# Delta rule: the products that complete the triangular inverse stand directly behind its blocks, ahead of the layout of queries and values and the grams

## The chip, the cores and the metric

The program runs on one core of one Trainium2 chip. The metric is device time in microseconds (us) of one execution. The engines are TensorE (PE, its weight loads PEld), VectorE (DVE), ScalarE (ACT), GpSimd (POOL) and SyncE (SP, which here issues the weight DMAs). Each runs its own instructions in its own fixed order and waits for the others by semaphores.

## The reference

One sequence of 256 tokens, width 1024, fp32, passes two blocks of two layers each. The first (differential attention with latent attention, then a dense network or a mixture of experts) isn't touched by the change. A layer of the second has grid attention beside a gated delta rule in both directions (8 heads, key and value width 64, chunks of 64 tokens), then a gated network with a convolution:

```python
k_beta = k * beta[..., None]
a_kk = where(strict, einsum("bhnid,bhnjd->bhnij", k_beta, k) * decay, 0.0)
t_inv = triangular_solve(eye + a_kk, eye, left_side=True, lower=True, unit_diagonal=True)
u = t_inv @ (v * beta);   w = t_inv @ (k_beta * exp(gcum))
qk = einsum("bhnid,bhnjd->bhnij", q, k) * decay
def step(state, inp):                     # over the chunks, in order
    v_new = ui - wi @ state
    o = qd @ state + qki @ v_new
    state = state * gt + kd.T @ v_new
```

q and k are normalised per head before (`l2norm`), and the two directions' outputs are added.

## The kernel before

A tile framework turns the Python code into one instruction list per engine. The order of the code is the priority; a list scheduler then places each instruction on its engine, by a model of times, when its inputs and its buffer are due. So the order on an engine is fixed before the run, isn't the order of the code, and can change far from an edit. PSUM tiles come from small rings: tag `sd` has 3 banks, `at` 2, `mm` 2, `ex` 1, and tiles of a tag are handed out in the order of the code.

The second block's weights stream in as 1 MB tiles `raw`. Most of its products are feature groups: `feat_group` multiplies a weight tile with the transposed activations `xf` in fp32 (L541, out `mm` or `ex`), or with split halves (L546 to L548). They depend on little and stand between everything else on PE.

`mix2` builds one mixer layer and steps through the generator `delta` with four calls of `next(dn)`, the last two directly behind each other (L1407, L1408). Behind them it writes down `dn_out` (which transposes the delta rule's output `O` into `odT`, L381 and L376/L377), the gates' groups (L541), the attention's output groups (on `oaT`) and the delta rule's (on `odT`).

`delta` goes, in the code's order, through these stages:

- decays and their exponentials; key layout and norm; per pair of heads (`hp`, 4 of them) the gram of the keys, and `apply` (L1680) which multiplies it into the decay matrix `Ma`;
- the inverse of all 64 x 64 unit triangles at once, on DVE: diagonal blocks of 32 are inverted by doubling and two closing passes (L1753, L1754), and two transposes (L1757) lay the blocks out as `xo`; copies bring them to `Wm` (L1762) and `Wc` (L1765), on ACT and DVE;
- weights of `qk` and `kd` on POOL;
- the part that the change moves (L1781 to L1788): `tok_layout(0)` and `tok_layout(2)` (transposes of `cT` on PE, copies on ACT, L1622), `l2norm(0, 0.125)` (queries: reductions L1629, small steps up to L1633 and products L1636 on DVE, transposes `cv` on PE, copies `qkT` L1640), and per pair of heads the gram of queries and keys and `apply` with `qk` on POOL (L1680);
- the loop that completes the inverse (L1789 to L1824): per pair of heads the tiles L1 (copies and transposes of `Ma`) and L2 (copies of `xo`, L1804), four products psY (L1808), the copy Yc (L1810, DVE), four products psZ (L1814), and the writing of the inverse into `Ma` (copies L1820, and psZ, L1823, L1824). psZ's products need Yc, and psY and psZ are `sd` tiles;
- `vf`, state and buffer clears (xv, L1836), and the recurrence: 16 pairs (hp, chunk), each a chain of products (L1865, L1887), copies and sums (L1860), staggered. L1665 and L1673 in the code are gram and its copies.

At the same time the grid attention runs in pieces, two heads at a time: scores (L1489), maximum (L1493), exponential `e` (L1498), transposes (L381), products (L1510), `ob` (L1514), and its transposes into `oaT` (L376, L377). Below, a step of a product group with its wait is written with the line that it has in this kernel; behind the change the lines L1789 to L1824 are 8 lower (L1808 is L1800, L1810 is L1802, L1814 is L1806, L1820 is L1812, L1801 is L1793, L1799 is L1791, L1804 is L1796).

Of the kernel before, what the change touches and what calls it, by code (L numbers as in the profile page):

```python
# [11 lines left out]
F32 = mybir.dt.float32  # L12
# [10 lines left out]
NT = 2  # L23
# [162 lines left out]
class Net:  # L186
# [1147 lines left out]
    def mix2(s, l):  # L1334
# [92 lines left out]
        for g in range(4):  # L1427
# [5 lines left out]
            nc.vector.tensor_tensor(out=v, in0=v, in1=m[:, gs, :], op=OP.add)  # L1433
            t = s.reg.tile([128, 2, 2, 256], F32R, tag=("E1", "E2", "KQ", "CV")[g], name="mT")
            s.split(t[:, 0], t[:, 1], v)
# [105 lines left out]
    def delta(s, l, cT, zb, sv, hg):  # L1541
        nc = s.nc
# [4 lines left out]
        reg, sm = s.reg, s.sm  # L1547
# [69 lines left out]
        def tok_layout(b3):  # L1617
            for tt in range(NT):
                pt = s.ps([128, 4, 128], "sd")
                for cc in range(4):  # L1620
                    s.tr(pt[:, cc], cT[b3 // 2][:, 4 * b3 % 8 + cc, tt * 128:tt * 128 + 128])
                nc.scalar.copy(cv[:, tt, b3].rearrange("p h d -> p (h d)"), pt.rearrange("p c d -> p (c d)"))  # L1622

        def l2norm(b3, scale):
            ss = sm.tile([128, NT, 8, 1], F32, tag="nss", name="nss")
            for tt in range(NT):
                j = s.tmp.tile([128, 8, 64], F32, tag="l0", name="j", bufs=2)
                nc.scalar.activation(j, cv[:, tt, b3], AF.Square)
                nc.vector.reduce_sum(ss[:, tt, :, 0], j, axis=AX.X)  # L1629
            TS(ss, ss, 4e-6, None, op0=OP.add)  # L1630
            r = s.rsqrt(ss, [128, NT, 8, 1])
            if scale != 1.0:
                TS(r, r, scale, None, op0=OP.mult)  # L1633
            for tt in range(NT):
                v = cv[:, tt, b3]
                T(out=v, in0=v, in1=r[:, tt].to_broadcast([128, 8, 64]), op=OP.mult)  # L1636
                pt = s.ps([128, 4, 128], "sd")
                for cc in range(4):
                    s.tr(pt[:, cc], cv[:, tt, b3, 2 * cc:2 * cc + 2].rearrange("p h d -> p (h d)"))
                nc.scalar.copy(qkT[:, b3, :, tt * 128:tt * 128 + 128], pt)  # L1640
# [9 lines left out]
        qk = reg.tile([128, 4, 4, 2, 64], F32, tag="qk", name="qk")  # L1650
# [13 lines left out]
        def gram(hp, w, out):  # L1664
            ps = [s.ps([128, 2, 128], "sd") for _ in range(2)]  # L1665
            for tt in range(NT):
                for h2 in range(2):
                    bs = slice(64 * h2, 64 * h2 + 64)
                    ts = slice(tt * 128, tt * 128 + 128)
                    mm(ps[h2][:, tt], lhsT=qkT[bs, 1, hp, ts], rhs=qkT[bs, w, hp, ts], start=True, stop=True)  # L1670
            for h2 in range(2):
                for hf in range(2):
                    nc.scalar.copy(out[H[hf], :, h2], ps[h2][H[hf], :, 64 * hf:64 * hf + 64])  # L1673

        def apply(d, kk, eng=nc.vector):
            for hf in range(2):
                for tt in range(NT):
                    n0 = (0, 1)[tt] if hf == 0 else (1, 0)[tt]
                    ns = slice(n0, 4, 3) if n0 == 0 else slice(1, 3)
                    eng.tensor_tensor(out=d[H[hf], ns], in0=kk[H[hf], tt:tt + 1].to_broadcast([64, 2, 2, 64]),  # L1680
                                      in1=d[H[hf], ns], op=OP.mult)
# [92 lines left out]
        for hp in range(4):  # L1774
            for hf in range(2):
                bw = ((1, 1), (3, 0)) if hf == 0 else ((0, 1), (2, 0))
                for ns, ts, k in ((slice(hf, 4, 2), slice(0, 2), 2),
                                  *((slice(n, n + 1), slice(t, t + 1), 1) for n, t in bw)):
                    PT(out=kd[H[hf], hp, ns], in0=cv[H[hf], ts, 1, h2s(hp)],
                       in1=eT[H[hf], ns, h2s(hp)].to_broadcast([64, k, 2, 64]), op=OP.mult)  # L1780
        tok_layout(0)  # L1781
        l2norm(0, 0.125)
        tok_layout(2)
        KQ = reg.tile([128, 4, NT, 2, 64], F32, tag="KQ", name="KQ")
        for hp in range(4):
            gram(hp, 0, KQ[:, hp])
            apply(qk[:, hp], KQ[:, hp], nc.gpsimd)
        yield  # L1788
        Ls = [reg.tile([128, 2, 2, 2, 128], F32, tag=tag, name="L") for tag in ("E1", "E2")]  # L1789
        for x in Ls:  # L1790
            nc.gpsimd.memset(x, 0.0)  # L1791
# [1 line left out]
        for hp in range(4):  # L1793
            hs = h2s(hp)
            L1, L2 = (x[:, hp % 2] for x in Ls)
            M = Ma[:, hp]  # L1796
            for hf in range(2):
                r0 = 64 * hf
                nc.scalar.copy(L1[r0 + 32:r0 + 64, :, :, r0:r0 + 32], M[r0 + 32:r0 + 64, hf::2, :, 0:32])  # L1799
                for n in (1 - hf, 3 - hf):  # L1800
                    nc.vector.transpose(out=L1[r0:r0 + 32, n // 2, :, r0 + 32:r0 + 64],  # L1801
                                        in_=M[r0 + 32:r0 + 64, n, :, 0:32])  # L1802
            for i in range(4):
                copies[i](L2[R32[i], :, :, 32 * i:32 * i + 32], xs(1, R32[i], i in (1, 2))[:, :, hs])  # L1804
            psY = s.ps([128, 2, 2, 32], "sd")
            for n in range(2):  # L1806
                for h2 in range(2):
                    mm(psY[:, n, h2], lhsT=L1[:, n, h2], rhs=Wm[:, n, 2 * hp + h2], start=True, stop=True)  # L1808
            Yc = s.tmp.tile([128, 2, 2, 32], F32, tag="m0", name="Yc")
            cp(Yc, psY)  # L1810
            psZ = s.ps([128, 2, 2, 32], "sd")
            for n in range(2):  # L1812
                for h2 in range(2):
                    mm(psZ[:, n, h2], lhsT=L2[:, n, h2], rhs=Yc[:, n, h2], start=True, stop=True)  # L1814
            for hf in range(2):
                r0 = 64 * hf
                nc.vector.memset(M[r0 + 32:r0 + 64, hf::2, :, 0:32], 0.0)
                nc.vector.memset(M[r0:r0 + 32, 1 - hf::2, :, 32:64], 0.0)
            for i in range(4):
                copies[i](M[R32[i], :, :, 32 * (i % 2):32 * (i % 2) + 32], Wc[R32[i], :, hs])  # L1820
            for hf in range(2):
                r0 = 64 * hf
                TS(M[r0:r0 + 32, hf::2, :, 32:64], psZ[r0:r0 + 32], -1.0, None, op0=OP.mult)  # L1823
                nc.scalar.mul(M[r0 + 32:r0 + 64, 1 - hf::2, :, 0:32], psZ[r0 + 32:r0 + 64], -1.0)  # L1824
        s.O = s.const.tile([128, NT, 8, 64], F32, tag="O", name="O")
        vf = reg.tile([128, NT, 8, 64], F32, tag="C4", name="vf")
        for tt in range(NT):
# [211 lines left out]
```

## Time and profile before

| | us |
|---|---|
| time, median of 3 runs (lowest to highest) | 2782.64 (2781.74 to 2784.24) |
| the profiled execution's own time | 2780.29 |
| its span, first to last instruction | 2778.5 |
| PE busy / PEld busy | 2668.2 (96%) / 2294.7 (83%) |
| DVE / ACT / POOL busy | 2081.2 (75%) / 1642.9 (59%) / 339.1 (12%) |
| mean granted clock of PE | 0.982 |

The delta rule stands in the span twice, at about 1855 to 2050 us and 2335 to 2530 us. A busy share is a mean over very different stages, so the stretches are read apart; a clock of 1.00 is full speed (2.4 GHz) and 0.50 half of it (1.2 GHz). In a row of the timeline the bracket at the end tells how long the engine stood idle before the instruction, and whose result ended that.

### The profile page before, as it was taken

The page shows a single profiled execution, that of the slowest core. Times are in us where ns is not written, and L with a number is a line of the kernel's source. Part 1 is how long each engine was busy: PE and PEld are TensorE (multiplying, and loading weights), DVE is VectorE, ACT ScalarE, POOL GpSimd, SP SyncE. Part 2 cuts the span into 40 slices and gives each one's busy share as a digit, 9 for nine tenths or more (in the row PEclk, how much of TensorE's full clock was granted, in tenths as well). Part 3 has the DMA queues.
Part 4 walks back from the last instruction along what each step waited for, and adds up shares of the span by engine and source line. Part 5 has one row for each costly group of instructions (what it writes and reads, how often), then busy time and mean ns, then how long its engine had stood idle before and what let it go on. Part 6 is the DMA issues. An engine that isn't in the chain of part 4 may idle for free. (4 is left out here: it accounts for less than half of the span.)

```text
span 2778.5 us, 41248 instructions
## 1 busy us (share of the span) xinstructions
PE 2668.2 (96%) x15729; PEld 2294.7 (83%) x15729; DVE 2081.2 (75%) x3322; ACT 1642.9 (59%) x2557; POOL 339.1 (12%) x360
## 2 busy tenths in 40 slices
PE   8999999899999999999999999989999999999999
PEld 7988998798887888788787878767788987777997
DVE  7576654647779989898988988869487856947784
ACT  5564543456467777777777777625555533455563
POOL 3324000132400000000000000024210003321000
PEclk9999999999989999999999999989999999999999
DMA  6335554433669999998999999532235543213553
GB/s 221 121 122 189 197 185 173 158 137 131 242 239 359 353 348 361 359 355 338 358 357 339 355 366 346 216 127 93 77 108 197 183 168 123 92 61 133 176 187 136
DMA packets 92939, 610.31 MB, mean 220 GB/s; under 512 B 13627, under 2 KB 14473, under 8 KB 22977
## 3 DMA queue, kind: packets, MB, share of 16 engines
q1 hardware_dynamic: 89968, 601.34, 58.8%
q0 software_dynamic: 2768, 6.28, 0.9%
q8 instruction: 126, 2.06, 0.3%
q14 instruction: 77, 0.62, 0.1%
HBM read 606.56 MB, written 1.05 MB: 219 GB/s over the span
## 5 line engine op out<-in xcount | busy, mean ns | idle before, releaser
L305 DVE TENSOR_TENSOR wl<-raw,wh 128x1024 fp32r<-128x1024 f32 (+1 forms) x938 | 1130.2, 1224 | 314.4 <-ACT wh L303 292.1
L303 ACT CAST wh<-raw 128x1024 fp32r<-128x1024 f32 (+1 forms) x996 | 1028.0, 1043 | 564.7 <-PE mm L342 162.4
L341 PE MATMUL mm<-wl,xg 128*128 128x512 f32 x896 | 354.8, 396 | 1.3
L340 PE MATMUL mm<-wh,xg 128*128 128x512 f32 x896 | 351.8, 395 | 0.0
L342 PE MATMUL mm<-wh,xg 128*128 128x512 f32 x896 | 351.1, 392 | 0.0
L547 PE MATMUL mm<-xTl,wh 128*128 128x256 f32 x1040 | 298.7, 287 | 0.0
L546 PE MATMUL mm<-xTh,wh 128*128 128x256 f32 x1040 | 297.6, 286 | 0.0
L548 PE MATMUL mm<-xTh,wl 128*128 128x256 f32 x1040 | 295.9, 285 | 0.4 <-DVE wl L305 0.4
L341 PEld LDWEIGHTS mm<-wl,xg 128*128 128x128 f32 x896 | 168.3, 188 | 42.4 <-DVE wl L305 7.4
L546 PEld LDWEIGHTS mm<-xTh,wh 128*128 128x128 f32 x1040 | 198.4, 191 | 1.9 <-issue 1.3
L548 PEld LDWEIGHTS mm<-xTh,wl 128*128 128x128 f32 x1040 | 198.7, 191 | 1.0 <-DVE wl L305 0.8
L340 PEld LDWEIGHTS mm<-wh,xg 128*128 128x128 f32 x896 | 168.3, 188 | 36.3
L547 PEld LDWEIGHTS mm<-xTl,wh 128*128 128x128 f32 x1040 | 197.7, 190 | 0.5
L342 PEld LDWEIGHTS mm<-wh,xg 128*128 128x128 f32 x896 | 168.3, 188 | 35.7
L305 POOL TENSOR_TENSOR wl<-raw,wh 128x1024 fp32r<-128x1024 f32 x58 | 143.0, 2466 | 332.8 <-ACT wh L303 324.8
L342 PE MATMUL sd<-wh,ac 128*128 128x512 f32 x448 | 175.6, 392 | 0.0
L341 PE MATMUL sd<-wl,ac 128*128 128x512 f32 x448 | 175.5, 392 | 0.0
L541 PE MATMUL mm<-xf,raw 128*128 128x256 f32 (+1 forms) x704 | 148.3, 361 | 0.0
L340 PE MATMUL sd<-wh,ac 128*128 128x512 f32 x448 | 144.2, 395 | 0.0
L541 PEld LDWEIGHTS mm<-xf,raw 128*128 128x128 f32 x704 | 119.0, 194 | 17.1 <-issue 3.7
L796 POOL DMA_DIRECT2D gb<-in_ln_ffn_g_dram x2 | 1.1, 561 | 971.6 <-DMA raw<-in_w_dram 971.3
L303 ACT CAST ww<-raw 128x1024 fp32r<-128x1024 f32 x74 | 77.2, 1047 | 67.2 <-PE mm L548 21.0
(627 smaller groups left out, 5452.4 us busy)
## 6 DMA issues: line engine op xcount, KB each, us to landing
raw<-in_w_dram SPq DMA_DIRECT2D x545, 1024.0 KB, 4.9
raw<-in_w_dram SPq DMA_DIRECT2D x24, 512.0 KB, 3.5
raw<-in_w_dram SPq DMA_DIRECT2D x8, 576.0 KB, 4.0
raw<-in_w_dram SPq DMA_DIRECT2D x8, 544.0 KB, 3.5
raw<-in_w_dram SPq DMA_DIRECT2D x4, 768.0 KB, 5.9
xt<-in_x_dram SPq DMA_DIRECT2D x2, 512.0 KB, 3.7
gb<-in_ln_mix_g_dram POOLq DMA_DIRECT2D x2, 512.0 KB, 4.9
gb<-in_ln_mix_b_dram POOLq DMA_DIRECT2D x2, 512.0 KB, 7.8
```

The costliest lines, as they stand in the source:

```text
L303: s.nc.scalar.copy(r[0], raw)
L305: eng.tensor_tensor(out=r[1], in0=raw, in1=r[0].bitcast(F32), op=OP.subtract)
L340: mm(out, lhsT=lh, rhs=rh, start=start, stop=False)
L341: mm(out, lhsT=lh, rhs=rl, start=False, stop=False)
L342: return mm(out, lhsT=ll, rhs=rh, start=False, stop=stop)
L541: mm(o[:, t], lhsT=h[:, kk, sl], rhs=xh[:, kk, t], start=kk == 0, stop=kk == k - 1)
L546: mm(o, lhsT=h[:, kk, sl], rhs=xh[:, kk, :], start=kk == 0, stop=False)
L547: mm(o, lhsT=h[:, kk, sl], rhs=xl[:, kk, :], start=False, stop=False)
L548: mm(o, lhsT=l[:, kk, sl], rhs=xh[:, kk, :], start=False, stop=kk == k - 1)
L796: s.nc.gpsimd.dma_start(gb[:, 0], row_bc(s.A[nm + "_g"], i * D, D))
```

## The change

The block of `delta` that lays out queries and values, normalises the queries and forms the grams of queries and keys moves behind the loop that completes the inverse. Nothing is added or left out.

```diff
@@ -1778,14 +1778,6 @@
                     PT(out=kd[H[hf], hp, ns], in0=cv[H[hf], ts, 1, h2s(hp)],
                        in1=eT[H[hf], ns, h2s(hp)].to_broadcast([64, k, 2, 64]), op=OP.mult)
-        tok_layout(0)
-        l2norm(0, 0.125)
-        tok_layout(2)
-        KQ = reg.tile([128, 4, NT, 2, 64], F32, tag="KQ", name="KQ")
-        for hp in range(4):
-            gram(hp, 0, KQ[:, hp])
-            apply(qk[:, hp], KQ[:, hp], nc.gpsimd)
-        yield
         Ls = [reg.tile([128, 2, 2, 2, 128], F32, tag=tag, name="L") for tag in ("E1", "E2")]
@@ -1822,6 +1814,14 @@
                 r0 = 64 * hf
                 TS(M[r0:r0 + 32, hf::2, :, 32:64], psZ[r0:r0 + 32], -1.0, None, op0=OP.mult)
                 nc.scalar.mul(M[r0 + 32:r0 + 64, 1 - hf::2, :, 0:32], psZ[r0 + 32:r0 + 64], -1.0)
+        tok_layout(0)
+        l2norm(0, 0.125)
+        tok_layout(2)
+        KQ = reg.tile([128, 4, NT, 2, 64], F32, tag="KQ", name="KQ")
+        for hp in range(4):
+            gram(hp, 0, KQ[:, hp])
+            apply(qk[:, hp], KQ[:, hp], nc.gpsimd)
+        yield
         s.O = s.const.tile([128, NT, 8, 64], F32, tag="O", name="O")
```

How this stands on the engines is taken from the two instruction lists. The first place is PE in the first layer, from the transpose of an attention block (`ob`) at the end of the inverse on. Before, feature groups and the transposes of the normalised queries (`cv`) and of `cT` follow:

```order
L381 MATMUL at<-ident,ob 128x128 [waits DVE_49]
L1489 MATMUL at<-AT 128x256 [waits PE_49]
L1489 MATMUL at<-AT 128x256
L541 MATMUL mm<-xf,raw 128x256 x4
L541 MATMUL ex<-xf,raw 128x256
L381 MATMUL sd<-ident,cv 128x128 [waits DVE_49]
L381 MATMUL sd<-ident,cv 128x128 x3
L381 MATMUL sd<-ident,cv 128x128 [waits DVE_49]
L381 MATMUL sd<-ident,cv 128x128 x3
L381 MATMUL sd<-ident,cT 128x128 x4
L541 MATMUL ex<-xf,raw 128x256 x9
```

With the change, from the same transpose on, psY (on `Wa` and `L`) and psZ (on `Yc`):

```order
L381 MATMUL at<-ident,ob 128x128 [waits DVE_49]
L1489 MATMUL at<-AT 128x256 [waits PE_49]
L1489 MATMUL at<-AT 128x256
L1800 MATMUL sd<-Wa,L 128x32 [waits DVE_49,Activation_49,Pool_49]
L1800 MATMUL sd<-Wa,L 128x32 x3
L1806 MATMUL sd<-Yc,L 128x32 [waits DVE_49,Activation_49,Pool_49]
L1806 MATMUL sd<-Yc,L 128x32 x3
L1800 MATMUL sd<-Wa,L 128x32 x4
L381 MATMUL at<-ident,e 128x128 [waits PE_49,Activation_49]
L381 MATMUL at<-ident,e 128x128
L381 MATMUL at<-ident,e 128x128 [waits Activation_49]
L381 MATMUL at<-ident,e 128x128
```

The four psY products and the four psZ products of the first pair now stand directly behind the attention's scores; the feature groups and the layout have gone behind all four pairs.

The second place is DVE in the same stretch, from the last copies into `Ma` on; before:

```order
L1820 COPY Ma<-Wa 32x8x32 x3
L1820 COPY Ma<-Wa 32x8x32 [waits DVE_49]
L1820 COPY Ma<-Wa 32x8x32 x3
L1493 TENSOR_REDUCE gnm<-at 128x2 [waits PE_49]
L377 TENSOR_TENSOR oaT<-at,oaT 128x4x128 [waits Activation_49]
L1495 TENSOR_TENSOR gnm<-gnm,gr 128x2 [waits DVE_49]
L1512 RECIPROCAL gsum<-gsum 128x2 [waits Activation_49]
```

With the change:

```order
L1812 COPY Ma<-Wa 32x8x32 x3
L1812 COPY Ma<-Wa 32x8x32 [waits DVE_49]
L1812 COPY Ma<-Wa 32x8x32 x3
L1493 TENSOR_REDUCE gnm<-at 128x2 [waits PE_49]
L1793 STREAM_TRANSPOSE L<-Ma 32x2x32 [waits PE_49]
L1793 STREAM_TRANSPOSE L<-Ma 32x2x32
L377 TENSOR_TENSOR oaT<-at,oaT 128x4x128 [waits Activation_49]
L1495 TENSOR_TENSOR gnm<-gnm,gr 128x2 [waits DVE_49]
L1802 COPY Yc<-sd 128x128 [waits PE_49]
L1793 STREAM_TRANSPOSE L<-Ma 32x2x32 x2
```

Yc of the first pair, which stood far behind the attention's steps, now comes behind the split of the attention's output (`oaT`, L377) and its small step L1495.

The third place is ACT beside it, from the last copies of the blocks on; before:

```order
L1804 COPY L<-xo 32x4x32 x2
L1820 COPY Ma<-Wa 32x8x32 x3
L376 CAST oaT<-at 128x4x128 [waits PE_49]
L1820 COPY Ma<-Wa 32x8x32 [waits DVE_49]
L1820 COPY Ma<-Wa 32x8x32 x3
L1417 ACTIVATE m<-mm 128x512 [waits PE_49]
L1640 COPY qkT<-sd 128x4x128 [waits PE_49] x2
```

With the change:

```order
L1796 COPY L<-xo 32x4x32 x2
L1812 COPY Ma<-Wa 32x8x32 x3
L1812 COPY Ma<-Wa 32x8x32 [waits DVE_49]
L1812 COPY Ma<-Wa 32x8x32 x3
L376 CAST oaT<-at 128x4x128 [waits PE_49]
L1791 COPY L<-Ma 32x4x32 [waits PE_49]
L1791 COPY L<-Ma 32x4x32
```

The cast to `oaT` (L376), for which DVE's L377 waits, stood between the copies into `Ma` and now stands behind all eight; the copies of `qkT` are gone from here.

The last place is PE behind the delta rule of the first layer, where its output `O` is transposed for the products on `odT`; before:

```order
L381 MATMUL sd<-ident,O 128x128 [waits DVE_49,Pool_49]
L381 MATMUL sd<-ident,O 128x128 [waits Pool_49] x3
L546 MATMUL mm<-oaT,wh 128x256
L547 MATMUL mm<-oaT,wh 128x256
L381 MATMUL sd<-ident,O 128x128 [waits DVE_49]
L381 MATMUL sd<-ident,O 128x128 x3
L548 MATMUL mm<-oaT,wl 128x256
```

With the change:

```order
L548 MATMUL mm<-oaT,wl 128x256
L381 MATMUL sd<-ident,O 128x128 [waits DVE_49,Pool_49]
L381 MATMUL sd<-ident,O 128x128 [waits Pool_49] x3
L381 MATMUL sd<-ident,O 128x128 [waits DVE_49]
L381 MATMUL sd<-ident,O 128x128 x3
L546 MATMUL ex<-odT,wh 128x256 [waits Activation_49]
L546 MATMUL mm<-odT,wh 128x256 [waits PE_49] x2
L547 MATMUL ex<-odT,wh 128x256 [waits DVE_49]
```

Before, products on `oaT` stand between and behind the two groups of transposes; now all eight transposes stand together, and the first products on `odT` directly behind them.

Behind it, 21 products L541 stand between the recurrence's first products in the first layer, where 1 stood before. The order of the weight DMAs on SP is the same in both lists. On POOL the two clears of `xv` (L1836) move ahead of the products into `vf` and `qk`.

## Rows read from the trace of the kernel before

**Rows 1.** Page, section 1, busy us and share of the span by engine

```profile
PE 2668.2 (96%) x15729; PEld 2294.7 (83%) x15729; DVE 2081.2 (75%) x3322; ACT 1642.9 (59%) x2557; POOL 339.1 (12%) x360
```

**Rows 2.** Stretches of both layers; busy us (instructions) of each engine, granted clock, DMA

```profile
1951.00:2011.00 60.00, 56.47 (x314) 47.40 (x314) 24.92 (x68) 32.98 (x86) 16.09 (x21) 0.94 0.21 71
...
2011.00:2050.00 39.00, 35.47 (x339) 26.19 (x340) 28.38 (x91) 21.14 (x77) 13.55 (x31) 1.00 0.12 44
...
2430.00:2489.00 59.00, 55.54 (x309) 46.58 (x309) 22.73 (x67) 31.86 (x84) 16.07 (x21) 0.94 0.15 54
...
2489.00:2530.00 41.00, 38.38 (x351) 28.26 (x352) 30.67 (x94) 23.51 (x81) 14.08 (x30) 1.00 0.17 54
...
2050.00:2070.00 20.00, 20.00 (x164) 19.79 (x163) 17.45 (x43) 8.79 (x11) 0.00 (x0) 1.00 0.38 125
...
2530.00:2550.00 20.00, 17.96 (x148) 17.52 (x148) 15.88 (x41) 7.97 (x10) 0.00 (x0) 1.00 0.47 158
```

**Rows 3.** Timeline, PE, first layer: start us, length us, instruction, idle before

```profile
1952.39 0.33 PE L381 MATMUL at<-ident,ob 128*128 128x128 f32 x1 [0.54 <-DVE ob L1514]
...
1964.02 0.66 PE L381 MATMUL sd<-ident,cT 128*128 128x128 f32 x4 [2.47 <-ACT qkT L1640]
...
2010.88 1.09 PE L1865 MATMUL sd<-xv,Ma 128*64 128x128 f32 x8
...
2013.78 0.68 PE L1887 MATMUL at<-xv,qk 128*64 128x64 f32 x8 [1.19 <-DVE xv L1874]
```

**Rows 4.** Timeline, DVE, first layer

```profile
1931.46 0.69 DVE L1629 TENSOR_REDUCE nss<-j 128x8 f32<-128x512 f32 x1
...
1951.98 0.17 DVE L1633 TENSOR_SCALAR rs_y<-rs_y 128x16 f32<-128x16 f32 x1
...
1952.26 3.08 DVE L1757 STREAM_TRANSPOSE xo<-X 128x1024 f32<-128x1024 f32 x2
...
1955.25 1.26 DVE L1636 TENSOR_TENSOR cv<-cv,rs_y 128x512 f32<-128x512 f32 x2
...
1957.19 1.26 DVE L1762 COPY Wa<-xo 32x512 f32<-32x512 f32 x2
...
1962.65 0.69 DVE L377 TENSOR_TENSOR oaT<-at,oaT 128x512 fp32r<-128x512 f32 x1
...
1991.39 0.27 DVE L1823 TENSOR_SCALAR Ma<-sd 32x128 f32<-32x128 f32 x1
...
1993.37 0.29 DVE L1810 COPY Yc<-sd 128x128 f32<-128x128 f32 x1
```

**Rows 5.** Timeline, ACT, first layer, the last row second layer

```profile
1953.53 2.19 ACT L1762 COPY Wa<-xo 32x512 f32<-32x512 f32 x2 [7.25 <-DVE xo L1757]
...
1960.95 0.58 ACT L376 CAST oaT<-at 128x512 fp32r<-128x512 f32 x1
...
1962.90 0.60 ACT L1417 ACTIVATE m<-mm 128x512 f32<-128x512 f32 x1
...
2431.53 2.21 ACT L1762 COPY Wa<-xo 32x512 f32<-32x512 f32 x2 [7.76 <-DVE xo L1757]
```

**Rows 6.** Timeline, PE, first layer, products of one pair of heads

```profile
1996.33 1.00 PE L1510 MATMUL at<-AT,eT 128*128 128x64 f32 x8
...
1997.17 1.03 PE L1814 MATMUL sd<-Yc,L 128*128 128x32 f32 x8
...
1998.03 1.06 PE L1808 MATMUL sd<-Wa,L 128*128 128x32 f32 x8
```

**Rows 7.** Timeline, PE, second layer, behind the delta rule

```profile
2543.19 0.50 PE L546 MATMUL mm<-odT,wh 128*128 128x256 f32 x2 [1.17 <-ACT odT L376]
```

**Rows 8.** Lines 1680 and 1860: count, duration ns min/median/max, first and last start

```profile
L1680 DVE TENSOR_TENSOR Ma<-kk,Ma x32: 349/836/4949, 1884.7 to 2381.5; 64x256 f32<-64x256 f32 x32
...
L1680 POOL TENSOR_TENSOR qk<-KQ,qk x32: 716/720/732, 1970.1 to 2463.7; 64x256 f32<-64x256 f32 x32
...
L1860 DVE TENSOR_TENSOR xv<-ck,cv x24: 271/287/577, 2019.3 to 2520.2; 64x128 f32<-64x128 f32 x24
```

## The prediction

> **What bounds the kernel now.** I read the engines' shares first: PE is busy for 96% of the span [rows 1], so the time is PE's work, which the change leaves alone, plus what PE waits and what it loses to a lower clock. Then the table of stretches around the two delta rules [rows 2]; the reader subtracts PE's busy time from each length. From the end of the inverse to the start of the recurrence PE stands 60.00 - 56.47 = 3.5 us in the first layer and 59.00 - 55.54 = 3.5 in the second; in the recurrence 3.5 and 2.6; behind it 0 and 2.0. In the first two stretches the granted clock is 0.94: if the lost part is a time at half clock, that costs 0.06 x 60 = 3.6 us and 0.06 x 59 = 3.5. All that a better order could take away around the inverse and the recurrence is thus 3.5 + 3.6 + 3.5 + 3.5 + 3.5 + 2.6 = 20.2 us, 0.7% of the time.
>
> Next PE's timeline: at the end of the inverse it waits 0.54 us for `ob` and 2.47 for `qkT` of ACT; the recurrence starts at 2010.88, with 1.19 for `xv` soon after [rows 3]. In between, feature groups L541 (which need nothing of the delta rule) fill PE while DVE and ACT work. And these are not quick: ACT copies from 1953.53 to 1962.90 without a break worth naming [rows 5], DVE transposes from 1952.26 and copies until L377 at 1962.65 [rows 4]. So around 1960 DVE and ACT are late and PE isn't, because it has other work in front of it. That is what the change turns round: psY and psZ, which need those copies, stand ahead of the feature groups.
>
> **The change part by part.** No instruction is added or removed, and no DMA changes its place on SP. The cost is in what PE, which keeps its order, meets first.
>
> *First psZ.* In the new order PE does the four psY products, then must wait for Yc, and everything else is behind it. When is Yc ready in the first layer? The queries' norm leaves DVE's way to the transposes: 2 reductions of 0.69 and 12 small steps of up to 0.17 [rows 4], 3.4 us by their lengths; short steps overlap their neighbours by some 0.05, and some may sit in gaps of others, so I take 2.5, between 1.4 (the reductions alone) and 3.4. `ob`, 0.2, goes behind the transposes. These then end at 1955.25 - 2.7 = 1952.6. ACT's copies start as much earlier, at 1950.8, and take the same 1962.90 - 1953.53 = 9.4 [rows 5]; L376 is now last of them, until 1960.2. DVE's L377 (0.69) waits for L376, Yc (0.29) stands behind L377: 1961.2 [rows 4]. On the other side, the copies to Wm end on DVE at 1957.19 + 1.26 - 2.7, less 1.3 for the queries' products L1636 which go, plus 0.2 for `ob`: 1954.7; four products step by 0.86 (from 1997.17 to 1998.03, [rows 6]): 1955.5. PE waits 5.7. If L377 didn't hold Yc, DVE would be there at 1962.65 - 2.7 - 1.3 + 0.2 = 1958.9 and Yc at 1959.2: 3.7, the low bound. In the second layer the copies start at 2431.53 - 2.5 [rows 5] and the same steps give the same distance, but a transpose of `e` (0.3, as the one of `ob` in [rows 3]) stands in front: 5.4.
>
> *Waits ahead of it.* `ob` comes at 1952.8 in place of 1952.39, while PE would be there at 1952.39 - 0.54 = 1951.9: 1.0 in the first layer, 0.5 in the second, where the order there stays as it was. For Wm another 0.4 in the first.
>
> *The other three steps.* From the reading of psZ on DVE (1991.39) to the end of the next Yc (1993.37 + 0.29) pass 2.3 us [rows 4]. PE has one group of psY (0.9) to do there, and where it is ready an attention product of 1.0 [rows 6]. So 0.4 to 1.4 a step, 1.2 to 4.2 for three; I take 2.6, in the middle, as both kinds stand in the new order. The clears of L, copies L1 and weights on POOL are far ahead of it.
>
> *Layout and grams behind.* They run in a row without feature groups, with three `sd` banks that ACT must empty: the trace has one such wait, the 2.47 at 1964.02 [rows 3], which came from ACT's queue. Between 0 and 2 a layer; I take 1.0. The clears of `xv` on POOL, past which `qk` moves, cost PE nothing unless POOL is late (rival below).
>
> *Behind the recurrence.* In the first layer all transposes of O now stand directly ahead of the products on `odT`. That is the order which the second layer has already, where PE waits 1.17 at the first [rows 7] and 20 - 17.96 = 2.0 in all, against 0 in the first [rows 2]: +2.0, once.
>
> *Clock.* Before, the granted clock is below full in the two stretches in which short waits stand between transposes and small products [rows 2]; there will be more of both. But part of the lower clock will lie inside the new waits, where it costs nothing. Between 0 and 3.6 a layer; I take 2.0.
>
> *What goes.* The feature groups that stood ahead come behind, and 21 of those products now stand inside the first rounds of the recurrence: its wait of 1.19 goes. So do the 3.5 + 3.6 of the first layer's stretch and the 3.5 + 3.5 of the second's.
>
> Sum: first layer 1.0 + 0.4 + 5.7 + 2.6 + 1.0 + 2.0 + 2.0 - 3.5 - 3.6 - 1.2 = +6.4; second 0.5 + 5.4 + 2.6 + 1.0 + 2.0 - 3.5 - 3.5 = +4.5. Together +10.9. The profiled execution would go from 2780.29 to 2791.2; it stands 2.35 below the median of the runs, so the median goes from 2782.64 to 2793.5. The time from one engine's end to the other's start isn't priced, which tilts it upward. With all bounds low (first psZ 3.7 and 3.4, three steps 1.2, no gram wait, no clock) it is 6.3 - 8.3 + 2.0 + 5.1 - 7.0 = -1.9, or 2780.7; with all high (steps 4.2, grams 2, clock 3.6), +10.9 + 2 x (1.6 + 1.0 + 1.6) = +19.3, or 2801.9.
>
> **The rivals.** *The waits are given back.* The feature groups that come later cover not only the first wait of the recurrence but all of them, 3.5 - 1.2 and 2.6 more, and hide the layout's and grams' waits (2.0): 10.9 - 4.9 - 2.0 = +4.0, and with the low end of the three steps (-2.8) +1.2: 2783.8, no change that can be told. For it: they are work without a condition. Against: 21 of the products must be enough, and the waits come where a round has no group in front.
>
> *It is faster.* Mechanism: Yc isn't held by L377, so the wait at the first psZ is 3.7, and the norm's 3.4 leave DVE fully; the clock no longer falls, since the layout is done in a block without pauses; and the recurrence, with its feature groups, has no wait. That is -1.9 - 0.9 x 2 - 4.9 = -8.6 with the bounds above: 2774.0. The point from which it decides is a sum of new waits under (20.2 - 2.0) / 2 = 9.1 us a layer. Against it: DVE keeps its order too, and L377 stands ahead of Yc.
>
> *Slower still, by POOL.* The 16 products into `qk`, 0.72 each on POOL [rows 8], are 11.5 us a layer. They can only begin once the grams are done, and now end inside the recurrence's first rounds, where DVE adds ck to two kinds of values (L1860, two inputs from SBUF). That line takes 271 to 577 ns, and DVE's own L1680, in another stretch, 349 to 4949 [rows 8]: there are executions in which something holds it. With +0.3 for each of the first round's 8, some 2.4 a layer: +10.9 + 4.8 = +15.7, or 2798.3; were `qk` itself late for L1887, up to 9 a layer, 2811. The Trainium skill, page SBUF — State Buffer, section "Who interferes with whom", says that a DVE instruction with two inputs in SBUF and a GpSimd instruction exclude each other over a shared port pair, for the whole instruction. By that rule the lengths above are blocked instructions, and the spread in the trace agrees with it (577 against a median of 287 ns).
>
> **How the numbers follow.** Forecast, the waits as summed: 0.57, its own range 2787 to 2800. Given back: 0.18. Faster: 0.11. Slower still: 0.14. The range of 2781 to 2803 leaves out most of the faster case and the top of POOL's. A measurement of this kernel tells about 0.2%, 5.6 us, from no change: faster is below 2777.1 (the faster case, 0.10), same reaches to 2788.2 (given back, and the low edge of the forecast, 0.22), slower has the rest, 0.68.
>
> **What would show it.** In the new trace: one wait of PE of 5 to 6 us in front of the first L1806 in each layer, ended by DVE's Yc, with L377 directly ahead of it on DVE; three waits near 0.9 at the next L1806; the recurrence's first rounds without waits; in the first layer a new wait of 1.2 ahead of L546 on `odT`. PE's busy time as before but for the clock. It is wrong if Yc's wait is under 3 us or the recurrence ends as much earlier as the inverse's end is late; and the POOL case is right if L1860 exceeds 0.5 us in the first rounds beside L1680 on POOL.

## The result, and the profile after

The changed kernel takes 2818.56 us (median of 4 runs, 2817.16 to 2820.59) against 2782.57 before: 36.0 us slower, a ratio of 1.0125 with a 95% interval of 1.0114 to 1.0137. The sign was forecast, the size was not: +10.9 with a range up to 2803. The profiled execution has a span of 2818.8, 40.3 above before's.

The first row of the page after, engine by engine, stands against [rows 1]:

```profile
PE 2695.0 (96%) x15729; PEld 2321.0 (82%) x15729; DVE 2087.0 (74%) x3322; ACT 1643.3 (58%) x2557; POOL 339.4 (12%) x360
```

PE does the same 15729 instructions, yet its busy time rises from 2668.2 to 2695.0, by 26.8. So two thirds of the 40.3 us are not waits: products take longer.

To see where, I cut both traces at the same places of PE's program: the starts of its instructions number 10240, 11200, 11600, 13100 and 14300, at which both kernels have done the same work. First before (stretch, length, PE busy and instructions, then PEld, DVE, ACT, POOL, the granted clock, DMA share and rate):

```profile
1892.20:2056.40 164.20, 151.79 (x962) 123.92 (x962) 116.62 (x315) 82.02 (x224) 46.52 (x79) 0.97 0.21 70
...
2056.40:2122.00 65.60, 61.61 (x403) 56.68 (x402) 51.98 (x85) 32.70 (x44) 1.48 (x2) 0.95 0.57 200
...
2122.00:2351.80 229.80, 228.34 (x1503) 204.10 (x1502) 156.38 (x291) 105.66 (x171) 15.86 (x22) 1.00 0.48 166
...
2351.80:2557.10 205.30, 189.67 (x1202) 155.42 (x1201) 148.64 (x355) 102.21 (x262) 61.45 (x97) 0.97 0.25 87
```

Then after, with the stretch at half clock as the last row:

```profile
1897.00:2073.20 176.20, 160.07 (x961) 130.89 (x961) 115.75 (x296) 81.64 (x224) 47.57 (x79) 0.91 0.19 65
...
2073.20:2148.00 74.80, 64.97 (x402) 59.61 (x401) 55.05 (x104) 33.81 (x46) 1.47 (x2) 0.89 0.48 170
...
2148.00:2379.60 231.60, 229.99 (x1503) 205.40 (x1503) 157.47 (x291) 104.74 (x169) 15.84 (x22) 0.99 0.47 167
...
2379.60:2599.30 219.70, 199.92 (x1201) 166.71 (x1200) 149.78 (x354) 101.45 (x261) 60.65 (x97) 0.90 0.24 79
...
1960.60:1991.30 30.70, 26.26 (x109) 23.79 (x110) 14.97 (x55) 16.40 (x47) 1.84 (x2) 0.50 0.00 1
```

The first stretch is the delta rule of the first layer with its recurrence: 176.2 - 164.2 = +12.0, of which busy time is 160.07 - 151.79 = +8.3 and waits +3.7. Behind it, around the transposes of O: +9.2, busy +3.4, waits +5.8. Between the layers +1.8. The second layer, all in one stretch: +14.4, busy +10.3, waits +4.2. These make 37.4; the two executions already stood 4.8 apart where the first stretch starts, and the rest runs 1.9 shorter. The last row tells why busy time grew: for 30.7 us PE ran at a granted clock of 0.50 (1.2 GHz), and it was busy for 26.26 of them. Before, the same stretch has 3.4 and 6.8 us at half clock. An estimate from these numbers: 26.26 us of work at half clock cost some 13 us, the 10.2 us of before at most 5, and the difference of 8 is about the +8.3. In the second layer the half clock lasts 34.1 us, from 2462.3 on, and PE is busy for 29.82 of them.

PE's timeline in that place, after (it answers to [rows 3]; L1800 is psY, L1806 psZ):

```profile
1958.55 0.33 PE L381 MATMUL at<-ident,ob 128*128 128x128 f32 x1 [3.02 <-DVE ob L1514]
...
1961.02 1.89 PE L1800 MATMUL sd<-Wa,L 128*128 128x32 f32 x8 [1.09 <-DVE Wa L1762]
...
1966.93 1.89 PE L1806 MATMUL sd<-Yc,L 128*128 128x32 f32 x8 [4.01 <-DVE Yc L1802]
...
1980.95 1.89 PE L1800 MATMUL sd<-Wa,L 128*128 128x32 f32 x8
...
1992.16 1.13 PE L541 MATMUL ex<-xf,raw 128*128 128x256 f32 x4
```

Three waits (3.02, 1.09, 4.01: 8.1 us) stand ahead of the first psZ. From there to the end of the steps PE has no wait, but a group of eight instructions takes 1.89 us, against 1.03 to 1.06 in [rows 6]. The clock is back only at 1991.3, just ahead of the first feature groups. DVE and ACT beside it:

```profile
1965.82 0.69 DVE L377 TENSOR_TENSOR oaT<-at,oaT 128x512 fp32r<-128x512 f32 x1 [0.29 <-ACT oaT L376]
...
1966.50 0.28 DVE L1802 COPY Yc<-sd 128x128 f32<-128x128 f32 x1
```

```profile
1962.84 2.34 ACT L1812 COPY Ma<-Wa 32x256 f32<-32x256 f32 x7
...
1965.20 0.58 ACT L376 CAST oaT<-at 128x512 fp32r<-128x512 f32 x1
```

ACT's seven copies L1812 end at 1965.18, L376 follows, DVE's L377 waits for it, Yc stands behind L377: the chain that the prediction named. In the second layer (PE, after):

```profile
2456.46 0.33 PE L381 MATMUL at<-ident,ob 128*128 128x128 f32 x1 [0.51 <-DVE ob L1514]
...
2462.15 1.71 PE L1800 MATMUL sd<-Wa,L 128*128 128x32 f32 x8 [2.81 <-DVE Wa L1762]
...
2468.14 0.66 PE L381 MATMUL at<-ident,e 128*128 128x128 f32 x2 [4.28 <-DVE oaT L377]
```

Here the wait of 4.28 stands at the transposes of `e`, ahead of psZ, and is ended by L377 itself; psZ behind them and the other steps have none.

At the end of the first layer's recurrence, PE and then DVE, after:

```profile
2085.14 1.94 PE L381 MATMUL sd<-ident,O 128*128 128x128 f32 x8 [5.03 <-DVE O L1533]
...
2087.75 0.58 PE L546 MATMUL ex<-odT,wh 128*128 128x256 f32 x1 [0.68 <-ACT odT L376]
```

```profile
2080.91 1.22 DVE L305 TENSOR_TENSOR wl<-raw,wh 128x1024 fp32r<-128x1024 f32 x1
...
2082.76 1.23 DVE L305 TENSOR_TENSOR wl<-raw,wh 128x1024 fp32r<-128x1024 f32 x1 [0.48 <-ACT wh L303]
...
2084.30 1.29 DVE L1533 TENSOR_TENSOR O<-O,rs_y 128x512 f32<-128x512 f32 x2
```

O's norm (small steps and, last, L1533) shares DVE with four weight splits L305, of which the last two are shown, and PE waits 5.03 us for O. From [rows 2] and [rows 7] I had expected 2.0 in all, for odT.

### The profile page after: what moved, and what is told of

Its sections match the earlier page's. It is cut to its first block, busy times and chain, and to the rows that moved or that the text cites. A ratio compares the mean times of both kernels' runs of the same rounds, so it can differ in the third digit from the quotient of the medians.

```text
span 2818.8 us, 41249 instructions
## 1 busy us (share of the span) xinstructions
PE 2695.0 (96%) x15729; PEld 2321.0 (82%) x15729; DVE 2087.0 (74%) x3322; ACT 1643.3 (58%) x2557; POOL 339.4 (12%) x360
## 5 line engine op out<-in xcount | busy, mean ns | idle before, releaser
L305 DVE TENSOR_TENSOR wl<-raw,wh 128x1024 fp32r<-128x1024 f32 (+1 forms) x938 | 1131.0, 1225 | 311.7 <-ACT wh L303 287.4
L548 PE MATMUL mm<-xTh,wl 128*128 128x256 f32 x1040 | 295.7, 284 | 0.4 <-DVE wl L305 0.4
L548 PEld LDWEIGHTS mm<-xTh,wl 128*128 128x128 f32 x1040 | 198.6, 191 | 1.0 <-DVE wl L305 0.8
L305 POOL TENSOR_TENSOR wl<-raw,wh 128x1024 fp32r<-128x1024 f32 x58 | 142.9, 2463 | 333.6 <-ACT wh L303 324.0
L541 PE MATMUL mm<-xf,raw 128*128 128x256 f32 (+1 forms) x704 | 145.8, 358 | 0.3 <-DVE cT L1312 0.3
L541 PEld LDWEIGHTS mm<-xf,raw 128*128 128x128 f32 x704 | 118.6, 193 | 16.1 <-issue 2.3
L305 DVE TENSOR_TENSOR ww<-raw,ww 128x1024 fp32r<-128x1024 f32 x74 | 90.2, 1223 | 42.1 <-ACT ww L303 41.3
```

The source lines that it names most:

```text
L305: eng.tensor_tensor(out=r[1], in0=raw, in1=r[0].bitcast(F32), op=OP.subtract)
L541: mm(o[:, t], lhsT=h[:, kk, sl], rhs=xh[:, kk, t], start=kk == 0, stop=kk == k - 1)
L548: mm(o, lhsT=l[:, kk, sl], rhs=xh[:, kk, :], start=False, stop=kk == k - 1)
```

## The experiments

Each kernel ran beside the kernel before. Its median was 2783.84 us beside the runs of one layer each, the first dummy products and the copies later; 2783.3 beside the norm of O, the pinned feature groups (both runs) and the copies alone; and 2782.57 beside the two groups of dummies and the last kernel. In brackets stands the ratio to it, with its 95% interval.

**One layer each.** The block as a function, called at the old place in one layer and at the new one in the other:

```diff
+        early = l == 1      # in the second run: l == 0
+        if early:
+            layout()
...
+        if not early:
+            layout()
```

> The block is moved in the first layer only; the second keeps the order of before. Theory CLOCK (the loss is PE at 1.2 GHz through the four steps of psY and psZ, set off by some 8 us of waits ahead of them, plus the late transposes of O in this layer): +12 us up to the recurrence and +9 at the transposes of O, some 2804 us; half clock of about 30 us in this layer alone. Rival WAITS (the loss is what PE waits for Yc and the steps, as in the prediction's sum): +6.4, some 2789.

> The block is moved in the second layer only. CLOCK: half clock of about 34 us there alone, +13 us, some 2796; the first layer as before. WAITS: +4.5, some 2787. If the two layers are independent, the gains or losses of this run and of the one with the first layer alone add up to the whole change, +36.

First layer 2805.64 (1.0079, 1.0063 to 1.0096): +21.8. Second 2797.97 (1.0053, 1.0036 to 1.0070): +14.1. Together 35.9 of 36.0: the layers are independent, and each costs more than three times the +6.4 and +4.5 of my sum. CLOCK's numbers (2804, 2796) are met, those of WAITS (2789, 2787) are not. But CLOCK had its numbers from the traces of the two kernels, so this shows that the loss stands in these stretches of each layer, and not yet what causes it.

**Work for nothing in the wait.**

```diff
...
             psZ = s.ps([128, 2, 2, 32], "sd")
+            if hp == 0:
+                with s.behind(last):          # the last psY product
+                    for _ in range(24):
+                        mm(psZ.rearrange("p n h c -> p (n h c)"), lhsT=s.ident, rhs=s.ident, start=True, stop=True)
```

> The whole change, and behind the first pair's psY 24 products of the identity with itself into the tile of psZ, which psZ overwrites: work for nothing, some 3.6 us at full clock in each layer, placed where PE stands still for Yc. CLOCK: PE is busy in the wait, so the half clock, 30.7 and 34.1 us in the changed kernel, ends far sooner, about 10 us a layer; the kernel gets faster by more work, by 5 to 12 us a layer: 2795 to 2808. WAITS: the wait is filled at best, no gain: 2818, or up to 2825 where the products run past Yc. A third theory, SMALL (products of 32 columns drop the clock by themselves, whatever stands ahead): the clock falls again in the steps, 2815 or more.

2811.77 (1.0107, 1.0090 to 1.0124; 2806.2 to 2813.45). PE, first layer, in the fastest of the four executions (2806.2; the dummies are L1807, psZ is L1810):

```profile
1956.98 1.89 PE L1800 MATMUL sd<-Wa,L 128*128 128x32 f32 x8 [1.13 <-DVE Wa L1762]
...
1958.68 6.39 PE L1807 MATMUL sd<-ident 128*128 128x128 f32 x34
...
1968.16 0.75 PE L1810 MATMUL sd<-Yc,L 128*128 128x32 f32 x6
...
1973.30 1.06 PE L1800 MATMUL sd<-Wa,L 128*128 128x32 f32 x8
...
1979.54 1.92 PE L1810 MATMUL sd<-Yc,L 128*128 128x32 f32 x8
```

The wait for Yc is gone. The 24 dummies were more work than the 3.6 us that I had set: their three rows in the trace make 8.4 us, in part at half clock. They start at half clock, which now ends after 6.8 us, and a later psY takes 1.06 where it had taken 1.89. At 1977.3 the clock falls once more, for 10.2 us, though PE has been busy without a pause in the 20.3 us since 1956.98: in this place the clock fell without a wait right ahead. That makes 17.0 us at half clock in place of 30.7. The centre is 6.8 us below the changed kernel's, but the intervals overlap, and the time lies between CLOCK's 2795 to 2808 and the 2818 of WAITS, so by itself this run doesn't decide.

**Two groups of it.** As above with 16 in each, the first group into the tile of psY behind the last attention product ahead of `ob`, at a high priority.

> The whole change, with 16 products of the identity with itself into the tile of the first psY, placed behind the last attention product ahead of the wait for ob, and 16 into the tile of the first psZ behind psY (both are overwritten): some 8 us of work for nothing in each layer, in front of and in the wait for Yc. CLOCK (the greater part of the loss is 1.2 GHz, set off by the waits ahead of the steps): with nearly no wait there the clock stays at 2.4 GHz through the steps, and in spite of the added work the time is 2788 to 2802. WAITS: the dummies at best fill the waits, 2815 or more. SMALL (the steps' small products drop the clock by themselves): half clock of 10 us or more in the steps although no wait stands ahead, 2803 to 2812.

2806.0 (1.0080, 1.0067 to 1.0094), clear of the changed kernel's interval: 12.6 us faster for 64 added products. PE, first layer (L1803 and L1813 are the dummies, L1806 psY, L1816 psZ):

```profile
1950.14 3.79 PE L1803 MATMUL sd<-ident 128*128 128x128 f32 x32
...
1958.14 0.47 PE L381 MATMUL at<-ident,ob 128*128 128x128 f32 x1 [3.35 <-DVE ob L1516]
...
1963.98 4.23 PE L1813 MATMUL sd<-ident 128*128 128x128 f32 x22
...
1969.64 1.38 PE L1813 MATMUL sd<-ident 128*128 128x128 f32 x10
...
1970.86 0.98 PE L1816 MATMUL sd<-Yc,L 128*128 128x32 f32 x8
...
1983.39 1.06 PE L1806 MATMUL sd<-Wa,L 128*128 128x32 f32 x8
```

And the stretches of both layers, from the same products as above:

```profile
1896.50:2066.60 170.10, 158.15 (x1026) 129.93 (x1025) 118.60 (x308) 82.09 (x224) 47.58 (x79) 0.97 0.19 67
...
2365.70:2584.70 219.00, 201.10 (x1265) 167.05 (x1264) 147.20 (x356) 102.96 (x263) 61.19 (x97) 0.94 0.24 83
```

In the first layer the half clock is down to 10.2 us, over before the first psZ, which takes 0.98; the stretch is 170.1 against 176.2, though 3.79 + 4.23 + 1.38 = 9.4 us of it is the dummies. An estimate: 20.5 us less at half clock save some 10, idle time falls by 16.1 - 11.9 = 4.2, the dummies add 9.4, which makes -5; measured are -6.1. So work for nothing paid here, by the clock. Another 5.5 of the 12.6 us stand elsewhere: around O the first layer's stretch is 69.30 against 74.80, because the wait of 5.03 for O isn't there in this order; no run shows that the dummies as work brought that. In the second layer the half clock at the steps is 17.0 us (10.2 and 6.8) in place of 34.1, but a wait of 4.97 for O with a half clock of 10.2 us has appeared, as the first layer had it, and the stretch is only 0.7 shorter.

The time came out above the 2788 to 2802 of my theory and inside the 2803 to 2812 of the third. The wait for `ob` stayed, 3.35. WAITS, as the whole of the loss, is refuted by this run. A clock that falls also without a wait is part of the truth: the 6.8 us in the second layer begin at 2469.0, and PE has been busy without a pause for 26.3 us by then. One thing is mixed in: the scheduler moved seven feature products from ahead of `ob` into the steps, so the run doesn't separate the missing wait from the feature products between the steps.

**Copies later.** The copies into Ma, which psZ doesn't need, were in front of L376 on ACT:

```diff
...
+                ends = (TS(M[r0:r0 + 32, hf::2, :, 32:64], ...), nc.scalar.mul(M[r0 + 32:r0 + 64, ...], ...))
             for i in range(4):
-                copies[i](M[R32[i], ...], Wc[R32[i], :, hs])
+                with s.behind(ends[i % 2]):
+                    copies[i](M[R32[i], ...], Wc[R32[i], :, hs])
```

> The whole change, with the copies of the diagonal blocks into Ma (8 on ACT, 2.7 us, and 8 on DVE, 1.9 us) held behind the use of psZ of their pair, so that they leave the way of Yc. WAITS: Yc comes 2.7 us earlier in each layer, 2818.6 - 5.4 = 2813. CLOCK: the waits ahead fall from 8.1 to about 5.4 us and the clock may still drop, with the half clock some 25 us: 2806 to 2813; if it doesn't drop, about 2795. LATER (the copies come back in the steps, which then wait for ACT and DVE): 2818 or more.

2812.82 (1.0106, 1.0090 to 1.0123). PE, first layer:

```profile
1965.75 1.89 PE L1806 MATMUL sd<-Yc,L 128*128 128x32 f32 x8 [2.50 <-DVE Yc L1802]
...
1979.78 1.89 PE L1800 MATMUL sd<-Wa,L 128*128 128x32 f32 x8
```

Yc's wait went from 4.01 to 2.50, and psY still takes 1.89: with 3.00 + 1.11 + 2.50 = 6.6 us of waits ahead the clock falls just the same, and for longer, 34.1 us. So the first stretch is only 1.0 shorter, 175.2. The time fits the 2813 of WAITS as well as the top of CLOCK's range, and doesn't tell them apart. Most of the difference of 5.7 us, whose interval overlaps the changed kernel's, stands elsewhere: around O the stretch is 69.1 against 74.8, again without the wait for O.

**The norm of O.** The splits of the weights for odT's products are held behind L1533 (`with s.behind(s.normed ...)` around the split of those four weights).

> The whole change, with the splits of the weights for the products on odT (on DVE) held behind the normalised O of the layer. Theory SPLITS (in the changed kernel three splits of 1.22 us stand on DVE between the small steps of O's norm, so PE waits 5.03 us for O and falls to 1.2 GHz for 10.2 us there): the wait shrinks to some 2 us, half clock there to 3 to 7 us, 2811 to 2816. Rival LATE WEIGHTS (the held splits are then late for the same products, and the wait only moves): 2818 or more.

2816.8 (1.0122, 1.0106 to 1.0137): 1.8 us, which can't be told from the changed kernel. PE (O's transposes are L383, the products L548 and L549):

```profile
2077.71 0.63 PE L383 MATMUL sd<-ident,O 128*128 128x128 f32 x4 [0.21 <-DVE O L1536]
...
2078.88 0.66 PE L383 MATMUL sd<-ident,O 128*128 128x128 f32 x4 [0.55 <-DVE O L1536]
...
2080.21 0.39 PE L548 MATMUL ex<-odT,wh 128*128 128x256 f32 x1 [0.68 <-ACT odT L378]
...
2082.35 0.58 PE L549 MATMUL ex<-odT,wh 128*128 128x256 f32 x1 [1.64 <-DVE odT L379]
```

The wait of 5.03 became 0.21 and 0.55, so the splits made most of it. But the odT split now waits behind the held ones, 1.64 more: holding them moves a third of the wait. The half clock there is 6.8 us, as SPLITS had set at most, and the stretch 71.3 against 74.8, but little of that is left in the time. Both theories were half right.

**Feature groups in the wait.** The same places filled with useful work: 28 products L541 of a layer get a high priority and a place behind the attention product (9), the first psY (10) and the later ones (3 each).

```diff
+                            p = s.pins.pop(0) if s.pins else None
+                            with nullcontext() if p is None else s.tc.high_priority(offset=s.PRIO), s.behind(p):
+                                mm(o[:, t], lhsT=h[:, kk, sl], rhs=xh[:, kk, t], start=kk == 0, stop=kk == k - 1)
```

> The whole change, with 28 products of the feature groups L541 per layer given a high priority and a place: 9 behind the last attention product in front of the wait for ob, 10 behind the first pair's psY, 3 behind each later psY. The four steps stay ahead of the layout and the grams. Theory COVER (what was lost is only that PE had nothing to do there, and then ran at 1.2 GHz): the waits of 8 us and the half clock of 30 us go, and the late transposes of O too, as groups no longer pile up at the end; 2775 to 2790. Rival ORDER (the steps ahead of the layout cost by themselves, as ACT and DVE are late): 2800 or more.

2817.64 (1.0125, 1.0110 to 1.0141): no gain; COVER's number is wrong, and the time is in the range of ORDER. PE, first layer (L544 is the feature group, L382 the transposes of `e`, L1807 psY, L1814 psZ), and DVE at that time:

```profile
1955.46 1.24 PE L382 MATMUL at<-ident,e 128*128 128x128 f32 x4 [7.37 <-ACT e L1502]
...
1963.19 6.17 PE L544 MATMUL ex<-xf,raw 128*128 128x256 f32 x14
...
1972.08 1.08 PE L1814 MATMUL sd<-Yc,L 128*128 128x32 f32 x8
```

```profile
1950.38 1.88 DVE L1759 TENSOR_TENSOR XP<-X,XP 128x1024 f32<-128x1024 f32 x1
...
1954.51 0.15 DVE L1499 TENSOR_TENSOR gnm<-gnm,gr 128x2 f32<-128x2 f32 x1
```

Where the groups stand, the theory holds: no wait before psZ, psZ of 1.08, full clock. But the attention's transposes of `e` came ahead, and PE waits 4.02 and 7.37 for `e`, in the second case because its maximum stands on DVE inside the inverse until 1954.66. At these waits the half clock lasts 17.1 us twice, from 1928.1 and 1952.0 on, 34.2 in place of 30.7, and the first layer's stretch is 178.1 against 176.2. So the work that can stand between was limited: put into one wait, it was missing in another.

> As the kernel with the pinned groups, with the copies into Ma held behind the use of psZ too. If Yc's wait is covered already, no difference to it, within 3 us; if the 10 products don't cover it, up to 3 us a layer faster.

2814.71 (1.0115, 1.0100 to 1.0131): 2.9 us below the run without it, within the 3 expected, and not to be told from it.

**The copies alone, on the kernel before.** The same edit without the move.

> The kernel before, with only the copies into Ma held behind the use of psZ, so that ACT can copy qkT earlier. If the wait of 2.47 us for qkT and the 6.8 us at half clock of each layer come from these copies: 2.5 + 3.4 us a layer less, some 2772. If something else is late instead or the clock falls anyway: within 3 us of before.

2771.98 (0.9956, 0.9943 to 0.9970): 11.3 us faster, where 11.8 were expected. PE in the first layer has kept one wait in this place:

```profile
1965.44 0.44 PE L381 MATMUL at<-ident,e 128*128 128x128 f32 x2 [1.77 <-ACT e L1498]
```

The wait of 2.47 for qkT [rows 3] is gone, 1.77 for `e` is there, and there is no half clock between 1935 and 2105. That the sum fits is luck all the same. The same stretches as above, of this kernel:

```profile
1895.10:2055.50 160.40, 148.92 (x961) 121.42 (x961) 119.13 (x312) 82.04 (x224) 46.79 (x79) 0.99 0.20 71
...
2055.50:2124.90 69.40, 62.42 (x403) 56.82 (x401) 52.36 (x87) 33.11 (x45) 1.48 (x2) 0.95 0.51 188
...
2354.70:2549.20 194.50, 186.03 (x1201) 153.29 (x1200) 146.44 (x355) 102.82 (x262) 61.25 (x97) 0.97 0.25 88
```

Against before the first layer wins 3.8 us and loses 3.8 around O, where waits of 1.06 and 0.75 for odT and of 1.03 have come. The gain, 10.8, stands in the second layer. There the 2.47 for qkT is gone too, but so are a wait of 4.62 for `eT` at 2387.2, ahead of these copies, and the 1.17 and 0.87 for odT: the held copies changed the scheduler's order farther than I had priced.

**And with cover for odT.** The last 12 products on oaT are held behind the transposes of O on PE (`s.behind(s.otr if tail and b == 1 else None)`).

> The kernel before with the copies into Ma held behind the use of psZ, and with the last 12 products on oaT held behind the transposes of O on PE, so that they cover the split into odT. If the waits of 1.2 and 0.9 us at the first products on odT in each layer are covered by them: 2 to 4 us less than with the held copies alone, some 2769. If the transposes then come too early for O: no difference, 2772.

2767.42 (0.9947, 0.9933 to 0.9960): 15.2 us faster than before, 51 faster than the change. Its interval overlaps that of the copies alone, so a gain by the cover isn't shown by the time. Both layers, the same products as above:

```profile
1894.60:2054.70 160.10, 148.91 (x961) 121.37 (x961) 118.84 (x312) 82.07 (x224) 46.96 (x79) 0.99 0.20 72
...
2350.50:2546.30 195.80, 186.01 (x1201) 153.24 (x1200) 146.84 (x355) 103.12 (x262) 61.14 (x97) 0.97 0.26 88
```

The first is 160.1 against 164.2 before, the second 195.8 against 205.3. Around O the first layer's stretch is 66.0, 3.4 less than with the copies alone, without their two waits for odT; the second layer had no such wait left to cover and is 1.3 longer.

## Why the prediction was right in its sign and wrong in its size

*What bounds it* was right: the same products, and time is what PE waits and what its clock loses.

*First psZ* was right in its chain, link by link. The waits came a little elsewhere: forecast 1.0 for `ob`, 0.4 for Wm, 5.7 for Yc, 7.1 in all; measured 3.02, 1.09 and 4.01, 8.1. In the second layer 0.5 and 5.4 were forecast, 0.51, 2.81 and 4.28 measured. Counted from the 4.8 us by which this execution was late, PE came to `ob` 1.1 us earlier and `ob` came 0.95 later than I had set: without the queries' norm DVE was done with the transposes 1.8 us sooner than before, where I had set 2.7.

*The other steps* failed in kind: I had PE wait 2.6 us at full clock. It waits nothing and works at half clock.

*Layout and grams behind*, 1.0 a layer: no wait showed between 1992 and 2018, and feature groups L541 do stand between them, which I had denied. *Recurrence*: the early rounds have no wait above 0.4, the later ones still wait, up to 0.63.

*Behind the recurrence*: forecast +2.0, measured +9.2 in that stretch. Its mechanism, an order like the second layer's, was not the one that decided: DVE's order of splits was, which the place of PE's transposes doesn't show, and 3.4 of the 9.2 are busy time again.

*Clock* is the step that failed by most. I took 2.0 a layer between 0 and 3.6, from the lost clock of [rows 2], and let 3.6 + 3.5 go: -3.1 in sum. Busy time in fact rose by 8.3 + 3.4 + 10.3 = 22.0 in the three stretches. My waits, by contrast, sum to 10.9 + 3.1 = 14.0, and 3.7 + 5.8 + 4.2 = 13.7 were measured. That these agree is luck: by stretch I had 6.0, 2.0 and 6.0. The bound of 3.6 was no bound: it was the loss in a stretch whose longest wait was 2.5 us, and I had no reason to take it for the most that longer waits can set off. I also priced the clock and the steps apart, though the work of the four steps is what was done at half clock: 26.26 us of it in the first layer, 29.82 in the second.

The trace of before had a longer wait, just ahead of the delta rule, in a stretch outside my rows. PE's timeline there, and the stretch at half clock around it, before:

```profile
1817.53 1.97 PE L381 MATMUL sd<-ident,h 128*128 128x128 f32 x8 [13.87 <-DVE h L1290]
```

```profile
1798.60:1822.50 23.90, 9.17 (x23) 6.33 (x24) 19.41 (x63) 4.95 (x12) 2.77 (x4) 0.50 0.22 69
```

The half clock lasts 23.9 us here, but the wait of 13.87 lies inside it and PE is busy for only 9.17: by estimate it cost some 4.6 us. That alone exceeds my bound of 3.6, yet it falls short of the 8.3 and 10.3 that were lost. No stretch of the trace before holds so much work at half clock, so the size could hardly be read from it; the upper end of the range should have been wider. Nor does the loss go with the length of the waits: with the copies later they were 6.6 in place of 8.1 us, and the half clock lasted 34.1 in place of 30.7.

*The rivals.* Given back and faster are refuted. POOL's didn't come to the test: the last product into `qk` ends on POOL at 2023.3 in the first layer and 2527.3 in the second, the first L1860 starts on DVE at 2034.1 and 2536.9. L1860 takes up to 573 ns after, 577 before, with medians of 290 and 287. Four of the long ones in the first layer (0.38 to 0.52 us, from 2042.5 to 2045.4) stand beside POOL's sums into O (L1900, 2041.8 to 2045.3), which the change leaves alone. That agrees with the Trainium skill's rule on the shared port (SBUF — State Buffer, "Who interferes with whom"), but the rule made no difference here.

What stays open: why DVE's splits come ahead of O's norm in some orders and not in others (the wait of about 5 us for O stands in the first layer of the changed kernel, in the second with the dummies and the pinned groups, and in neither with the copies later), and what lets the clock fall, and stay low, in the steps. The waits ahead aren't all of it, as the falls without one show; no run has the small products alone.

## What to carry to other kernels

A dependent chain moved forward on an engine that runs in order, and is nearly always busy, takes away the work that stood in front of it. Here the last psZ came 28 us sooner, counted from the start of the first stretch, and the recurrence still started 3.2 us later. So list for each wait of the chain what independent work will stand there. Price a wait twice: for its own length, and for the work that would run at 1.2 GHz behind it; where the trace before has no row with so much work at that clock, say that the term is open and widen the range. Split a difference by stretches of the same work before calling a forecast right: two sums here fitted although their parts didn't. And look at the copies first: holding 16 copies a layer that nobody waited for yet brought 11.3 us, where moving the whole stage lost 36.

## What the runs showed of the hardware that was not expected

Work for nothing made a stretch faster: with 9.4 us of added products the first layer's took 170.1 us in place of 176.2, as 20.5 us at half clock went. (The kernel with 64 such products took 12.6 us less, of which 5.5 stand elsewhere.) The clock of 0.50 lasted 30.7 us while PE was busy for 26.26 of them, and at 1977.3 in the first dummy run it fell though PE had been busy without a pause for 20.3 us.
